# State-space chunks on one core: outputs made as features by tokens in column halves, the decay mask on ScalarE, two banks of transposes

## Chip, cores and metric

The kernel runs on one NeuronCore of one Trainium2 chip. The metric is the time of one launch in device microseconds, the median over several runs of the same kernel. A core has TensorE for matrix products and transposes, VectorE, ScalarE and GpSimd for element work, and SyncE, which here does nothing but start transfers. Products land in PSUM, which has eight banks of 512 float32 columns on 128 partitions; each `[P, 512]` tile below is one bank.

## What is computed

One inference step of a two-layer model: a Mamba-2 state-space (SSD) layer, then a Griffin (RG-LRU) layer, each followed by a squared-ReLU MLP. There are 16 meta tokens and 1024 prompt tokens, and beside them 8 sample tokens with states of their own. The change touches the SSD layer's recurrence over the prompt alone. It runs in chunks of 128 tokens (the 16 meta tokens are a short chunk in front), with 8 groups of 4 heads, 64 features a head and 128 states:

```python
cs = jnp.cumsum(ac, axis=2)                     # a: log decays, per token and head
Lmat = segsum_exp(jnp.moveaxis(cs, 2, -1))      # exp(cs_l - cs_s) where s <= l, else 0
cb = jnp.einsum("bclgn,bcsgn->bcgls", Cc, Bc)
scores = cb[:, :, :, None] * Lmat
y_diag = jnp.einsum("bcgrls,bcsgrp->bclgrp", scores, x)           # x is x * dt
decay_to_end = jnp.exp(cs[:, :, -1:] - cs)
chunk_states = jnp.einsum("bcsgn,bcsgrp->bcgrpn", Bc, x * decay_to_end[..., None])
# h_next = h * exp(cs_last) + chunk_states, h_prev is the state ahead of a chunk
y_off = jnp.einsum("bclgn,bcgrpn->bclgrp", Cc, h_prev) * jnp.exp(cs)[..., None]
y = y_diag + y_off                              # then y + x * d_skip, times silu(z), group norm, w_out
```

Everything around it (projections, convolution, gates, norms, MLPs) is the same in both kernels.

## The kernel before

**Layout.** Activations stand with features on partitions and tokens along the columns. For a group g, `x0` and `x1` are the 2 x 128 features of its four heads after the convolution, `Bf` and `Cf` the 128 state columns; in the trace all four are called `conv`. The result `yf` has the same layout, 2 x 128 features by tokens.

**Order of work.** The SSD layer goes group by group. `ssd_group(g)` is a generator; each step of it (a slot) issues one stage of each of three consecutive chunks. Between the slots the loop over groups advances a second generator, `fill(g)`, which issues the projection of the next group's x, B and C columns and of this group's gate z: bundles of 24 float16 products (8 tiles of the inner dimension, three passes of high and low parts) into one of the four banks `mm0` to `mm3`. The trace calls them `mm<-U,wh`. Further lanes run beside them: the group norm of the group before, and the conversion of weights to float16 parts. The instructions are then placed on their engines by a scheduler that honours data dependences, so the order on an engine isn't exactly that of the code. Every engine call passes through a helper, so nearly every row of the trace names line 89 and is told apart by its tiles.

**A chunk.** Its work in three stages, in the slots i, i+1 and i+2:

- `spread`, a slot earlier: SyncE starts one transfer (line 1017) that copies the chunk's cumulative sums from the DRAM tile `csd` to all 128 partitions, as `L`, 4 heads x 128 columns.
- `pe_a`, `ew_a`: TensorE transposes `x0`, `x1` and `Bf` into the bank `tp` and multiplies B by C into the bank `cb`. VectorE subtracts each token's own sum from `L` and caps at 0 (four instructions, `L<-L,ncs`); ScalarE takes the exponential; VectorE makes `xdt` = x dt and `xdd` = x dt exp(cs_last - cs) out of `tp`, then `cbm` = `cb` times the triangle, then `L` = `L` times `cbm`. ScalarE copies B's transpose to `Bt`.
- `pe_b`, `ew_b`: TensorE makes the chunk's state `st` (`xdd` by `Bt`), and in the bank `yo` the part from the carried state (`hst` by C, tokens on partitions, 256 columns) and four products of `xdt` and `L`, 64 columns each. GpSimd multiplies the carried state by its decay, VectorE adds `st`: the next `hst`. VectorE makes `yt` = first half of `yo` times `es` (exp of the sums, a column per head), and adds the second half.
- `pe_c`, `ew_c`: TensorE transposes `yt` back into free columns of `cb`; VectorE adds x times D and writes `yf`.

`tp`, `cb`, `st` and `yo` have one bank each: the next chunk's products into a bank wait until the last reader of the bank is done. `L`, `xdt`, `xdd`, `yt` and `hst` have two buffers each. In slot 1 the sample tokens' B and C go by way of DRAM to all partitions (`row`, `bcd`, `bc`), in slots 3 to 6 VectorE and GpSimd work on the sample tokens' states, and slot 8 ends them. A float32 product shows as two passes in the trace (f32 x2).

Of the kernel before, what the change touches and what calls it, by code (L numbers as in the profile page):

```python
# [10 lines left out]
F32 = mybir.dt.float32  # L11
# [10 lines left out]
P = 128  # L22
# [55 lines left out]
class Queue:  # L78
    """An engine; while hold is set its instructions are issued in program order, and later ones behind them."""
# [38 lines left out]
class Body:  # L118
# [18 lines left out]
    def tab(self, *args, **kw):  # L137
        """An activation whose function needs a table set: these stay in program order."""
# [13 lines left out]
    # ---------------------------------------------------------------- setup  # L152
    def setup(self):
# [28 lines left out]
        # pre-norm gains and group-norm gains scaled by a power of two so that hi/lo fit float16  # L182
# [13 lines left out]
        # the inputs of the ffn leave room for sums of four  # L196
# [13 lines left out]
        self.csd = self.dram.tile([288, P], F32, name="csd")  # L210
        self.bcd = [self.dram.tile([8, 2, P], F32, name=f"bcd{i}") for i in range(2)]
# [33 lines left out]
    def pow2(self, b, n, pool, tag):  # L245
        """p = the power of two at or below b; s = 2^14 / p."""
# [9 lines left out]
    # -------------------------------------------------------------- weights  # L256
# [14 lines left out]
    def split(self, w, st, s, parts):  # L271
        """w = float16 hi and lo parts of st * s, s [P, parts] by contiguous column ranges."""
# [12 lines left out]
    def wconv(self, st, kind, cols=SW):  # L285
        """A strip of weights as float16 hi and lo parts [P, 2, KT, cols], the factor that undoes its scaling and,
        for kinds h and H, the factor of its hidden units. Kind a takes a bound from the sums of the magnitudes, kind s
        one that kind g found before; kinds 2 and S carry the factors of the hidden rows. Kinds H and S are for the
        products by Winograd's form: with the quarters that are used as they are."""
# [50 lines left out]
    def quarter(self, s, inv):  # L340
        """Scales that leave room for sums of four."""
# [101 lines left out]
    def summed(self, b, s):  # L443
        """Whether the hidden units of a strip of block b enter the second product by Winograd's form."""
# [7 lines left out]
    def bundle(self, ps, w, m, act, c, kts=range(KT), first=True, last=True):  # L452
        """ps += sum over k of w[k, m tile]^T act[k, chunk c], three passes of the float16 parts."""
# [14 lines left out]
    def new_u(self):  # L468
        """Float16 parts of the normed input by chunk and k tile."""
# [28 lines left out]
    def normed(self, x, ss, i, hi, lo, pool):  # L498
        """Steps: the pre-norm i of a chunk (its k tiles in x), as float16 parts in hi and lo [P, KT, n]."""
# [15 lines left out]
    def boundary(self, m, ss, xc, piece, ipost, xdst, ipre, U, pool):  # L515
        """Steps: x + norm(m) for a piece of a chunk to xdst; then its pre-norm."""
# [37 lines left out]
    def last_phase(self, ws, act, ipost, xsrc, xdst, ipre, evac, pre=None, split0=None):  # L554
        """The last product before a norm, chunk by chunk; the norms of a chunk run beside the next one."""
# [47 lines left out]
    def first_phase(self, strips, act, evac):  # L603
        """Products of the first strips after a norm: chunk 2 of the input comes last."""
# [15 lines left out]
    # ------------------------------------------------------------------ SSD  # L620
    def ssd(self):
# [5 lines left out]
        with tc.tile_pool(name="dts", bufs=1) as dts:  # L627
            with tc.tile_pool(name="rows", bufs=1, reuse_waits="tile") as rows, \
# [23 lines left out]
                for g in range(G):  # L652
# [5 lines left out]
                    nslot = 13  # L658
# [29 lines left out]
    def start_x(self, c):  # L688
        """A chunk of the input, in the room of later rows: its k tiles, and room left over."""
# [25 lines left out]
    def start_norm(self, U, c, x, sq, ufs):  # L715
        """Steps: the first pre-norm of a chunk."""
# [942 lines left out]
```

## Time and profile before

| what | value |
|---|---|
| median of 3 runs | 2834.31 us (2834.26, 2834.31, 2837.87) |
| span of the profiled execution | 2836.7 us, 56933 instructions |
| its own time beside the span | not recorded apart; the span is 2.4 us over the median |
| mean granted TensorE clock | 0.968 |
| TensorE products busy | 2583.1 us (91%) |
| VectorE busy | 2110.1 us (74%) |
| ScalarE busy | 1322.6 us (47%) |
| GpSimd busy | 691.4 us (24%) |
| DMA | 229.15 MB, mean 81 GB/s |

"Busy" is the time in which the engine executes something; what it waits for is told by other views. A row of the timeline begins with start and length in us and ends, in brackets, with a wait and what ended it. A row of a group of instructions has, between bars, its total busy time and the mean ns of one, and then the idle time ahead of it. A row by windows has for each engine the busy us and the count of instructions, then the granted clock as a share of the full one, the share of time in which the DMA engines are busy, and GB/s.

### The profile page before, as it was taken

Reading aid. Unit: us, or ns where it says so; the run is one execution under the profiler, and the core shown is the slowest. Engines: PE = TensorE matmul, PEld = TensorE weight load, DVE = VectorE, ACT = ScalarE, POOL = GpSimd, SP = SyncE. Lnnn points to the kernel's source line nnn. Section 1 sums busy time; section 2 is a strip of 40 time slices with the busy share of each in tenths; the row PEclk is TensorE's granted clock in tenths of the full one; section 3 lists DMA queues with packets and bytes.
Section 4 is the critical chain, followed back from the end, with each engine's and each line's share of the span. In section 5 each row is a group of like instructions: output and inputs, shape, how many; then the busy total and the mean of one; then the engine's idle time right before and its main releaser. Section 6 shows DMA issues by size and latency. Waiting matters only on the chain. (4 is left out here: it accounts for less than half of the span.)

```text
span 2836.7 us, 56933 instructions
## 1 busy us (share of the span) xinstructions
PE 2583.1 (91%) x23209; PEld 2060.6 (73%) x23209; DVE 2110.1 (74%) x5043; ACT 1322.6 (47%) x2148; POOL 691.4 (24%) x972
## 2 busy tenths in 40 slices
PE   4999999999999999789989999979999779989998
PEld 2666666666666667789989976646667779989976
DVE  4889778977873685568778788787685667878776
ACT  4655455545544354344253344658564335253352
POOL 2222111212212024442232201123014452231301
PEclk9999999999999999889999999989999989999999
DMA  3232233223345320101122123110220101111122
GB/s 123 99 119 90 87 107 115 102 88 108 113 159 187 117 106 31 46 31 46 61 72 79 46 110 113 63 62 33 89 108 31 46 31 46 47 45 53 54 73 95
DMA packets 52758, 229.15 MB, mean 81 GB/s; under 512 B 9056, under 2 KB 18416, under 8 KB 31632
## 3 DMA queue, kind: packets, MB, share of 16 engines
q1 hardware_dynamic: 46112, 190.81, 19.1%
q0 software_dynamic: 6384, 34.71, 3.1%
q8 instruction: 181, 2.97, 0.4%
q14 instruction: 81, 0.66, 0.1%
HBM read 186.28 MB, written 39.22 MB: 79 GB/s over the span
## 5 line engine op out<-in xcount | busy, mean ns | idle before, releaser
L89 PEld LDWEIGHTS <-wh 128*128 128x128 f16 x17040 | 1504.0, 99 | 503.7 <-issue 54.7
L89 PE MATMUL mm<-U,wh 128*128 128x350 f16 (+3 forms) x7056 | 989.4, 297 | 20.7 <-ACT rr L89 13.2
L89 PE MATMUL mm<-H,wh 128*128 128x175 f16 (+5 forms) x5664 | 557.7, 253 | 35.3 <-DVE z L89 30.4
L89 PEld LDWEIGHTS <-wp 128*128 128x128 f16 x3888 | 311.0, 99 | 87.6 <-issue 60.5
L89 POOL TENSOR_TENSOR ws<-ws 128x256 f32<-128x256 f32 (+1 forms) x192 | 205.2, 1069 | 328.6 <-DVE wp L89 214.4
L89 DVE TENSOR_TENSOR z<-z,mm 128x175 f32<-128x175 f32 (+3 forms) x648 | 228.4, 370 | 29.2 <-ACT z L89 22.0
L89 POOL PARTITION_ALL_REDUCE wgb<-rm x100 | 55.5, 555 | 656.6 <-issue 338.4
L89 PE MATMUL mm<-U,wp 128*128 128x175 f16 (+1 forms) x1728 | 154.8, 245 | 55.2 <-DVE z L89 55.1
L89 PE MATMUL mm<-TT,wh 128*128 128x175 f16 (+1 forms) x1728 | 167.0, 248 | 10.2 <-ACT TT L89 9.3
L89 ACT ACTIVATE z<-z,ti 128x700 f32<-128x700 f32 (+1 forms) x72 | 63.0, 875 | 183.5 <-DVE z L89 183.5
L89 DVE SCALAR_TENSOR_TENSOR wh<-ws,sw,wh 128x1024 f16<-128x1024 f32 x94 | 122.0, 1320 | 28.3 <-ACT wh L89 28.3
L89 DVE TENSOR_SCALAR qw<-wgb 128x1 f32<-128x1 f32 x103 | 15.5, 150 | 167.3 <-POOL wgb L89 167.1
L89 DVE SCALAR_TENSOR_TENSOR wh<-ws,s,wh 128x256 f16<-128x256 f32 x256 | 114.7, 490 | 11.1 <-ACT wh L89 11.1
L89 DVE TENSOR_REDUCE rm<-ws 128x1 f32<-128x2048 f32 x40 | 91.3, 2281 | 31.2 <-DMA ws<-w 26.7
L89 PE MATMUL mm<-H,wp 128*128 128x175 f16 (+1 forms) x864 | 90.5, 241 | 25.5 <-DVE z L89 23.1
L89 DVE TENSOR_TENSOR ss<-ss,sqt 128x350 f32<-128x350 f32 (+3 forms) x154 | 75.9, 500 | 41.8 <-ACT sqt L89 41.1
L89 ACT ACTIVATE wh<-ws,s 128x512 f16<-128x512 f32 x128 | 83.0, 710 | 48.0 <-POOL ws L89 23.2
L89 DVE SCALAR_TENSOR_TENSOR conv<-pre,ssmall,conv 128x1072 f32<-128x1072 f32 x78 | 103.8, 1330 | 0.1
L89 ACT ACTIVATE wh<-ws,sw 128x2048 f16<-128x2048 f32 x47 | 93.7, 1993 | 14.5 <-DVE sw L89 11.7
L89 DVE TENSOR_SCALAR L<-L,ncs 128x128 f32<-128x128 f32 (+1 forms) x288 | 90.6, 357 | 13.2 <-DMA L<-csd 13.2
L89 DVE TENSOR_TENSOR H<-z,H 128x175 f16<-128x175 f32 (+5 forms) x120 | 81.2, 694 | 23.6 <-ACT H L89 19.5
L89 ACT ACTIVATE pre<-mm,undo 128x8 f32<-128x8 f32 (+1 forms) x104 | 46.5, 474 | 110.7 <-PE mm L89 110.7
(279 smaller groups left out, 4176.9 us busy)
## 6 DMA issues: line engine op xcount, KB each, us to landing
ws<-w SPq DMA_DIRECT2D x64, 1024.0 KB, 4.9
ws<-w_ssd_in SPq DMA_DIRECT2D x24, 1024.0 KB, 5.4
L<-csd SPq DMA_DIRECT2D x64, 256.0 KB, 3.2
ws<-w_lru_in SPq DMA_DIRECT2D x12, 1024.0 KB, 4.9
xd<-xc POOLq DMA_DIRECT2D x6, 1400.0 KB, 5.5
xc<-xd SPq DMA_DIRECT2D x6, 1400.0 KB, 6.0
h<-ssd_h SPq DMA_DIRECT2D x8, 1024.0 KB, 4.9
bc<-bcd SPq DMA_DIRECT2D x8, 1024.0 KB, 4.8
```

Source lines behind the costliest of these rows:

```text
L89: r = f(*args, **kw)
```

## The change

1. `y` is made directly as features by tokens. The part from the carried state becomes two products of 128 columns, with two heads of `hst` stationary and C moving. The four products of `xdt` and `L` exchange their operands: `xdt` (64 columns) is stationary, `L` (128 columns) moves, and head h lands on partitions 0 to 63 or 64 to 127 of `yo`, by h modulo 2. The two transposes of `yt`, and the third stage with them, are gone; a group has 10 slots of chunk work and `nslot` is 12.
2. The exponentials of the sums, formerly columns `es`, are now needed along the tokens: they are written to a second DRAM tile, `esd`, and spread over the partitions by two transfers a chunk into `ex`, issued by SyncE in `spread`. VectorE multiplies the first half of `yo` by `ex`; GpSimd adds that to `yf`, into which VectorE has written x D + the second half of `yo`.
3. The mask: four Relu on ScalarE of cs - `L` (scale -1, the sum as bias), then the exponential with scale -1, in place of four instructions on VectorE.
4. `tp` alternates between two banks (those formerly `tp` and `cb`), and B C goes to its last 128 columns.

```diff
+        self.esd = self.dram.tile([288, P], F32, name="esd")
...
-                    nslot = 13
+                    nslot = 12
...
-        ncs = dts.tile([P, 9, 32], F32, name="ncs")
-        nc.vector.tensor_scalar(f(ncs), f(cs), -1.0, None, op0=OP.mult)
+        esr = dtt.tile([96, 3, 128], F32, name="esr")
+        self.tab(esr, csr, AF.Exp)
+        nc.sync.dma_start(self.esd.rearrange("(i p) c -> p i c", i=3), esr)
...
-        es = dts.tile([P, 9, 32], F32, name="es")
-        self.tab(f(es), f(cs), AF.Exp)
...
-        nc.vector.tensor_tensor(f(dd), f(ncs), tps[:, :288], op=OP.add)
+        nc.vector.tensor_tensor(f(dd), tps[:, :288], f(cs), op=OP.subtract)
...
-        def pe_a(i, cb):
+        def pe_a(i):
...
-            tp = psp.tile([P, 512], F32, tag="tp", name="tp")
+            tp = psp.tile([P, 512], F32, tag=("tp", "cb")[i % 2], name="tp")
...
-            nc.tensor.matmul(cb[:Q, :Q], Bf[:, es], Cf[:, es], start=True, stop=True)
+            nc.tensor.matmul(tp[:Q, 384:384 + Q], Bf[:, es], Cf[:, es], start=True, stop=True)
...
             nc.sync.dma_start(L[:Q, :, :Q], self.csd[None, r:r + 4, :Q].to_broadcast([Q, 4, Q]))
             S["L", i] = L
+            if i:
+                ex = tmp.tile([P, 2, 128], F32, tag="yt", name="ex", bufs=2)
+                for h in range(2):
+                    nc.sync.dma_start(ex[64 * h:64 * h + 64], self.esd[None, r + h:r + 4:2].to_broadcast([64, 2, 128]))
+                S["ex", i] = ex
...
             for h in range(4):
-                nc.vector.tensor_scalar(L[:Q, h, :Q], L[:Q, h, :Q], self.ncs[:Q, tt, 4 * g + h:4 * g + h + 1], 0.0,
-                                        op0=OP.add, op1=OP.min)
-            self.tab(L[:Q, :, :Q], L[:Q, :, :Q], AF.Exp)
+                nc.scalar.activation(L[:Q, h, :Q], L[:Q, h, :Q], AF.Relu, scale=-1.0,
+                                     bias=self.cs[:Q, tt, 4 * g + h:4 * g + h + 1])
+            self.tab(L[:Q, :, :Q], L[:Q, :, :Q], AF.Exp, scale=-1.0)
...
             if i:
-                nc.tensor.matmul(yo[:, :256], Cf[:, es], fl(hst[0]), start=True, stop=True)
+                for t in range(2):
+                    nc.tensor.matmul(yo[:, 128 * t:128 * t + 128], fl(hst[0][:, 2 * t:2 * t + 2]), Cf[:, es], start=True,
+                                     stop=True)
             for h in range(4):
-                nc.tensor.matmul(yo[:Q, 256 + 64 * h:320 + 64 * h], L[:Q, h, :Q], xdt[:Q, h], start=True, stop=True)
+                p, o = 64 * (h % 2), 256 + 128 * (h // 2)
+                nc.tensor.matmul(yo[p:p + 64, o:o + Q], xdt[:Q, h], L[:Q, h, :Q], start=True, stop=True)
...
                 nc.gpsimd.tensor_tensor(hn, hst[0], self.ecd[:, tt, hs, None].to_broadcast([P, 4, 64]), op=OP.mult)
                 nc.vector.tensor_tensor(fl(hn), fl(hn), st[:, :256], op=OP.add)
-                nc.vector.tensor_tensor(yt.rearrange("p (h d) -> p h d", h=4),
-                                        yo[:, :256].rearrange("p (h d) -> p h d", h=4),
-                                        self.es[:, tt, hs, None].to_broadcast([P, 4, 64]), op=OP.mult)
-                nc.vector.tensor_tensor(yt, yt, yo[:, 256:], op=OP.add)
...
-        def pe_c(i, cb):
-            Q = dims(i)[0]
-            yt = S.pop(("y", i))
-            for t in range(2):
-                nc.tensor.transpose(cb[:, 128 + 128 * t:128 + 128 * t + Q], yt[:Q, 128 * t:128 * t + 128],
-                                    ident[:Q, :Q])
...
             for t in range(2):
                 nc.vector.scalar_tensor_tensor(yf[:, t, c0:c0 + Q], xs[t][:, es], v["dsk"][:, 2 * g + t:2 * g + t + 1],
-                                               cb[:, 128 + 128 * t:128 + 128 * t + Q], op0=OP.mult, op1=OP.add)
+                                               yo[:, 256 + 128 * t:256 + 128 * t + Q], op0=OP.mult, op1=OP.add)
+            if i:
+                ex = S.pop(("ex", i))
+                nc.vector.tensor_tensor(fl(ex), yo[:, :256], fl(ex), op=OP.mult)
+                nc.gpsimd.tensor_tensor(yf[:, :, c0:c0 + Q], yf[:, :, c0:c0 + Q], ex, op=OP.add)
```

The rest of the diff removes comments.

The order of the instructions moves with it. The numbers behind the names of tiles are buffers; `conv_2896` (before) and `conv_2881` (after) are the same group's C, `conv_2269`, `conv_2520`, `conv_2730` its x0, x1, B (after: `conv_2265`, `conv_2468`, `conv_2726`). On TensorE, one chunk's block in the middle of the third group, before:

```order
L89 MATMUL cb_3320<-ident_83,yt_3265 128x128 x2
L89 MATMUL st_3323<-xdd_3271,Bt_3279 128x256
L89 MATMUL yo_3325<-hst_3264,conv_2896 128x256
L89 MATMUL yo_3325<-xdt_3270,L_3162 128x64 x4
L89 MATMUL tp_3331<-ident_83,conv_2269 128x128
L89 MATMUL tp_3331<-ident_83,conv_2520 128x128
L89 MATMUL tp_3331<-ident_83,conv_2730 128x128
L89 MATMUL cb_3320<-conv_2896,conv_2730 128x128
```

and after:

```order
L89 MATMUL st_3312<-xdd_3260,Bt_3268 128x256
L89 MATMUL yo_3314<-conv_2881,hst_3252 128x128 x2
L89 MATMUL yo_3314<-L_3149,xdt_3259 64x128 x4
L89 MATMUL tp_3321<-ident_83,conv_2265 128x128
L89 MATMUL tp_3321<-ident_83,conv_2468 128x128
L89 MATMUL tp_3321<-ident_83,conv_2726 128x128
L89 MATMUL tp_3321<-conv_2881,conv_2726 128x128
```

The transposes of `yt` are gone, the two products into `yo` have their operands exchanged, and all that the next chunk's first stage needs comes out of one bank. Between two such blocks of a group stand 24 to 49 projection products after the change.

On SyncE, the same group's transfers in the order in which they are issued, before:

```order
L1017 DMA L_3162<-csd_142 128x512
L1090 DMA bcd0_143<-row_3198 8x256
L1093 DMA bc_3201<-bcd0_143 128x2048
L1017 DMA L_3244<-csd_142 128x512
L1017 DMA L_3318<-csd_142 128x512
L1017 DMA L_3413<-csd_142 128x512
L1017 DMA L_3487<-csd_142 128x512
```

and after:

```order
L1023 DMA ex_3235<-esd_143 64x2x128 x2
L1018 DMA L_3307<-csd_142 128x512
L1018 DMA L_3428<-csd_142 128x512
L1023 DMA ex_3309<-esd_143 64x2x128 x2
L1023 DMA ex_3430<-esd_143 64x2x128 x2
L1018 DMA L_3509<-csd_142 128x512
L1018 DMA L_3609<-csd_142 128x512
L1018 DMA L_3694<-csd_142 128x512
L1023 DMA ex_3511<-esd_143 64x2x128 x2
```

`L_3307` and `ex_3309` belong to one chunk, `L_3428` and `ex_3430` to the next, `L_3509` and `ex_3511` to the one behind: `ex` of a chunk stands behind `L` of up to two later chunks.

On ScalarE, the middle of the same group, after (before, one exponential of `L` stands in the place of each row of Relus and the exponential behind it):

```order
L89 ACTIVATE L_3307<-L_3307,cs_945 128x128 x3
L89 ACTIVATE L_3307<-L_3307 128x512
L89 ACTIVATE pre_3355<-mm_3402,undo_3105 128x350
L89 ACTIVATE ysp_3142<-yf_2039 128x2x350
L89 ACTIVATE L_3428<-L_3428,cs_945 128x128 x2
L89 ACTIVATE Bt_3463<-tp_3442 128x128
L89 ACTIVATE L_3428<-L_3428,cs_945 128x128 x2
L89 ACTIVATE L_3428<-L_3428 128x512
```

`Bt_3463` belongs to the chunk of `L_3307`; it now stands behind the first Relus of the next chunk's `L_3428`, which wait for the landing of its sums.

More of the change, by code (lines that the diff above doesn't have):

```diff
@@ L840, in dt_phase @@
         self.dtfm, self.decfm = fm
-        self.dt, self.cs, self.ncs, self.ecd, self.es, self.dtd = dt, cs, ncs, ecd, es, dtd
+        self.dt, self.cs, self.ecd, self.dtd = dt, cs, ecd, dtd
     def softplus(self, out, x, pool, n, parts=1):
@@ L1018, in spread, with ew_a @@
             S["L", i] = L
-        def ew_a(i, tp, cb):
+            if i:
[3 more added lines that the diff above has]
+                S["ex", i] = ex
+        def ew_a(i, tp):
             Q, tt, es, _ = dims(i)
@@ L1034, in ew_a @@
             cbm = tmp.tile([P, 128], F32, tag="cbm", name="cbm", bufs=2)
-            nc.vector.tensor_tensor(cbm[:Q, :Q], cb[:Q, :Q], tri[:Q, :Q], op=OP.mult)
+            nc.vector.tensor_tensor(cbm[:Q, :Q], tp[:Q, 384:384 + Q], tri[:Q, :Q], op=OP.mult)
             nc.vector.tensor_tensor(L[:Q, :, :Q], L[:Q, :, :Q], cbm[:Q, None, :Q].to_broadcast([Q, 4, Q]),
@@ L1046, in pe_b @@
             if i:
-                nc.tensor.matmul(yo[:, :256], Cf[:, es], fl(hst[0]), start=True, stop=True)
+                for t in range(2):
+                    nc.tensor.matmul(yo[:, 128 * t:128 * t + 128], fl(hst[0][:, 2 * t:2 * t + 2]), Cf[:, es], start=True,
+                                     stop=True)
             for h in range(4):
-                nc.tensor.matmul(yo[:Q, 256 + 64 * h:320 + 64 * h], L[:Q, h, :Q], xdt[:Q, h], start=True, stop=True)
+                p, o = 64 * (h % 2), 256 + 128 * (h // 2)
+                nc.tensor.matmul(yo[p:p + 64, o:o + Q], xdt[:Q, h], L[:Q, h, :Q], start=True, stop=True)
             return st, yo
         def ew_b(i, st, yo):
-            Q, tt, es, _ = dims(i)
+            Q, tt, es, c0 = dims(i)
             hn = tmp.tile([P, 4, 64], F32, tag="hst", name="hst", bufs=2)
-            yt = tmp.tile([P, 256], F32, tag="yt", name="yt", bufs=2)
             if i == 0:
                 nc.vector.tensor_copy(fl(hn), st[:, :256])
-                nc.vector.tensor_copy(yt[:Q], yo[:Q, 256:])
             else:
@@ L1061, in ew_b @@
                 nc.vector.tensor_tensor(fl(hn), fl(hn), st[:, :256], op=OP.add)
-                nc.vector.tensor_tensor(yt.rearrange("p (h d) -> p h d", h=4),
-                                        yo[:, :256].rearrange("p (h d) -> p h d", h=4),
-                                        self.es[:, tt, hs, None].to_broadcast([P, 4, 64]), op=OP.mult)
-                nc.vector.tensor_tensor(yt, yt, yo[:, 256:], op=OP.add)
-            hst[0] = hn
-            S["y", i] = yt
-        def pe_c(i, cb):
-            Q = dims(i)[0]
-            yt = S.pop(("y", i))
-            for t in range(2):
-                nc.tensor.transpose(cb[:, 128 + 128 * t:128 + 128 * t + Q], yt[:Q, 128 * t:128 * t + 128],
-                                    ident[:Q, :Q])
-        def ew_c(i, cb):
-            Q, tt, es, c0 = dims(i)
             for t in range(2):
                 nc.vector.scalar_tensor_tensor(yf[:, t, c0:c0 + Q], xs[t][:, es], v["dsk"][:, 2 * g + t:2 * g + t + 1],
-                                               cb[:, 128 + 128 * t:128 + 128 * t + Q], op0=OP.mult, op1=OP.add)
+                                               yo[:, 256 + 128 * t:256 + 128 * t + Q], op0=OP.mult, op1=OP.add)
[3 more added lines that the diff above has]
+                nc.gpsimd.tensor_tensor(yf[:, :, c0:c0 + Q], yf[:, :, c0:c0 + Q], ex, op=OP.add)
+            hst[0] = hn
         def sample_bc():
@@ L1126, in ssd_group @@
         spread(0)
-        for i in range(n + 2):
+        for i in range(n + 1):
             if i + 1 < n:
                 spread(i + 1)
-            cb = psp.tile([P, 512], F32, tag="cb", name="cb")
-            if 0 <= i - 2 < n:
-                pe_c(i - 2, cb)
-            if 0 <= i - 1 < n:
+            if i:
                 rb = pe_b(i - 1)
             if i < n:
-                ra = pe_a(i, cb)
-            if 0 <= i - 2 < n:
-                ew_c(i - 2, cb)
-            if 0 <= i - 1 < n:
+                ra = pe_a(i)
+            if i:
                 ew_b(i - 1, *rb)
             if i < n:
-                ew_a(i, ra, cb)
+                ew_a(i, ra)
             if i == 1:
```

## The prediction

> **What bounds the kernel now.** I read first the busy times of three stretches of the span, the middle one being the state-space chunks (from the first group's slots to the last's), because only there does the change touch anything.
>
> ```profile
> span 2836.7 us, 56933 instructions
> core 0: us, PE busy (x) PEld busy (x) DVE busy (x) ACT busy (x) POOL busy (x), PEclk, DMA share, GB/s
> 115.90:850.00 734.10, 696.82 (x4642) 491.02 (x4641) 601.42 (x1679) 371.62 (x571) 154.46 (x259) 0.98 0.31 109
> 392.90:487.90 95.00, 89.90 (x611) 63.10 (x610) 78.31 (x213) 48.98 (x77) 19.47 (x35) 1.00 0.29 103
> ```
>
> The stage takes 734 us. TensorE is busy for 697 of them, 95%; VectorE for 601, 82%; ScalarE for 372, 51%; GpSimd for 154, 21%. The last row is one group of heads, 95.0 us, with the same shares. So TensorE sets the pace, and VectorE is close behind. TensorE's idle time is 734.1 - 696.8 = 37.3 us, and the granted clock of 0.98 stands for about 0.02 x 734 = 15 us of further loss. Second I read whom TensorE waits for in that stretch (total us, times, longest):
>
> ```profile
> PE cb L89 <- DVE cbm L89: 12.8, 9, 3.0
> PE yo L89 <- DVE yt L89: 7.1, 5, 2.8
> PE yo L89 <- DVE L L89: 6.6, 3, 3.2
> PE st L89 <- DVE hst L89: 4.8, 6, 1.1
> PE st L89 <- ACT Bt L89: 2.6, 7, 1.4
> ```
>
> Four rows name VectorE: 12.8 + 7.1 + 6.6 + 4.8 = 31.3 of the 37.3 us. A saving thus comes in two ways: fewer TensorE cycles in a chunk (worth their full length) and fewer of these waits. Third, the order of time on TensorE in an undisturbed chunk (start, length of the merged row, which overlaps the next row by the tail of the last matmul, so starts are what I subtract):
>
> ```profile
> 406.48 0.38 PE L89 MATMUL cb<-ident,yt 128*128 128x128 f32 x2
> 406.70 0.60 PE L89 MATMUL st<-xdd,Bt 128*128 128x256 f32 x2
> 407.13 0.59 PE L89 MATMUL yo<-hst,conv 128*128 128x256 f32 x2
> 407.56 1.00 PE L89 MATMUL yo<-xdt,L 128*128 128x64 f32 x8
> 408.40 0.50 PE L89 MATMUL tp<-ident,conv 128*128 128x128 f32 x3
> 408.74 0.39 PE L89 MATMUL cb<-conv 128*128 128x128 f32 x2
> 408.96 3.72 PE L89 MATMUL mm<-U,wh 128*128 128x350 f16 x24
> ```
>
> A chunk's block is 2.48 us (406.48 to 408.96), and a bundle of 24 projection products follows. There are 8 groups x 8 full chunks = 64 blocks. Each float32 product stands as two passes.
>
> **The change on TensorE.** (1) The two transposes of `yt` go: 406.48 to 406.70, 0.22 x 64 = 14 us. They stand on TensorE itself, so this counts in full. (2) The product with the carried state was one of 256 columns in two passes, 0.43 us (407.13 to 407.56); it becomes two of 128 columns, four passes. The `cb<-conv` row, 128 columns in two passes, takes 0.22, so four take 0.44: nothing. (3) The products of mask and x exchange their operands: eight passes with 64 moving and 128 stationary columns become eight with 128 moving and 64 stationary ones, in halves of the array that alternate. Now they take 0.84 (407.56 to 408.40), 0.105 a pass. One after the other, the new ones take 8 x 0.11 = 0.88, a loss of 0.04; with the two halves fully beside each other half of that, a gain of 0.40. No row shows two halves at work. Changes of the array's layout have two near rows, in a group's first chunk:
>
> ```profile
> 394.70 0.69 PE L89 MATMUL st<-xdd,Bt 16*128 16x256 f32 x2 [0.21 <-ACT Bt L89]
> 395.32 0.61 PE L89 MATMUL yo<-xdt,L 16*16 16x64 f32 x8
> 396.25 0.39 PE L89 MATMUL cb<-conv 128*128 128x128 f32 x2
> 396.47 0.38 PE L89 MATMUL mm<-ident,conv 128*8 128x128 f32 x2
> 396.69 0.61 PE L89 MATMUL mm<-U,wh 128*128 128x350 f16 x3
> ```
>
> Going to 8 stationary columns and back costs nothing: 0.22, as the row before it. Going from `st` to 16 rows takes 0.62 from start to start where two such passes take 0.43, so a change costs at most 0.19. Two changes a block give a worst end of 0.04 + 0.38 = 0.42 x 64 = 27 us lost; the best end is 0.40 x 64 = 26 us gained. The 8-column row is the nearest (columns are narrowed here too), so I put changes at nothing and the halves between 0 and 26, at 10 gained: the two passes of a head must follow each other, so only neighbours of different heads can meet.
>
> The Trainium skill ("TensorEngine Tiling (Array Packing)", Key Properties) says that a change of tiling mode drains the engine, and that tiles run in parallel. The 0.22 above shows no drain. By the parallel part alone this term would be 26; by the drain alone it would lie towards the other end.
>
> **The change on the other engines.** (4) VectorE loses the four subtractions that prepare the mask and the two steps that make `yt`, and gains one product with the spread exponentials `ex`.
>
> ```profile
> 406.91 0.87 DVE L89 TENSOR_SCALAR L<-L,ncs 128x128 f32<-128x128 f32 x4
> L89 DVE TENSOR_TENSOR yt<-yo,es 128x256 f32<-128x256 f32 x64 | 26.7, 417 | 18.0 <-issue 9.6 <-PE yo L89 5.6 <-ACT wh L89 2.6
> L89 DVE TENSOR_TENSOR yt<-yt,yo 128x256 f32<-128x256 f32 x64 | 26.1, 409 | 0.0
> L89 POOL TENSOR_TENSOR hst<-hst,ecd 128x256 f32<-128x256 f32 x64 | 42.1, 658 | 125.3 <-DVE hst L89 51.4 <-DVE ysp L89 22.0 <-PE mm L89 15.6
> L89 ACT ACTIVATE Bt<-tp 128x128 f32<-128x128 f32 x64 | 17.3, 270 | 23.4 <-DVE xdd L89 22.9
> ```
>
> Per chunk 0.87 + 0.42 + 0.41 - 0.42 = 1.28 us, x 64 = 82 us less of VectorE's 601. (5) GpSimd gains one addition of 128x256 a chunk, priced as its state product: 64 x 0.66 = 42 us, on an engine at 21%. It stands in GpSimd's queue beside the state product that the next chunk needs; the states stand ahead of the additions there in most places, so I charge nothing directly. But GpSimd holds VectorE up:
>
> ```profile
> 455.05 3.61 POOL L89 TENSOR_TENSOR h<-h,decfm 128x2048 f32<-128x2048 f32 x1 [1.98 <-DMA h<-ssd_h]
> 455.13 3.55 DVE L89 SCALAR_TENSOR_TENSOR yf<-conv,ssmall,ys 128x8 f32<-128x8 f32 x1
> ```
>
> An 8-column operation takes 3.55 us because a GpSimd product runs beside it. The new additions may hold VectorE between 0 and 42 us in all; I take 8, since VectorE is reading PSUM, or idle, for much of a chunk. So VectorE gets about 74 us back. The Trainium skill ("GPSIMD Engine Reference", Key points) states the rule: GpSimd shares its SBUF interfaces with VectorE, in the way of operations with two SBUF inputs. The pair of rows agrees; were every addition to fall on such an operation, the relief would be 40 instead of 74.
>
> (6) ScalarE gains four Relu of 128x128 a chunk. Priced as `Bt`, of that size: 4 x 0.27 = 1.08, x 64 = 69 us, and it would be busy 441 of some 690 us, 64%. That is hidden as long as a chunk's exponentials are done before its mask is needed, one bundle and one block later (3.7 + 2.5 = 6.2 us); relu and exp take 1.08 + 0.63. What is queued behind the first Relu, which waits for its rows to land, are `Bt` and the copies out of the projection's banks; `Bt` is what TensorE's `st` waits for. (7) SP gets two more transfers a chunk. The landing time is that of the present rows:
>
> ```profile
> L<-csd SPq DMA_DIRECT2D x64, 256.0 KB, 3.2
> ```
>
> They move 128 KB a chunk, half of that row. SP issues nothing else that the chunks wait for but `L`, so the issuing is hidden; their place in the queue is the first rival below. The stage's DMA share is 0.31, so bandwidth is no limit. (8) `tp` with two banks and no `cb`: the first wait of the list above, 12.8 us, is the wait for the single bank of `cb`, and loses its cause. Late next is what stands behind it in the same chunk, `st` and `yo`, which still have one bank each and are freed by VectorE. (9) The start-up gains one exponential and one small transfer and loses a multiplication and an exponential: nothing. (10) One slot fewer (12 for 13) only moves projection products among slots.
>
> **The waits.** Their ends are 0 (VectorE still too late in the slots that also carry the sample tokens, the convolution and the group norm) and 31 + 15 = 46 us (all of VectorE's share and of the clock's). VectorE gives back 74 us, more than twice its 31, but TensorE becomes shorter too, and the heavy slots stay heavy: I take about half, 24 us.
>
> **Sum.** 14 + 0 + 10 + 24 = 48 us; the second bank of `tp` has no entry beside its part of the waits. The profiled execution's span is 2836.7; the runs shown are 2834.26, 2834.31 and 2837.87, so the span lies 2.4 above their median, and nothing else of that execution's time is recorded. 2836.7 - 48 = 2788.7 by the profile, 2834.3 - 48 = 2786 on the scale of the median.
>
> **Rivals.**
> A. The late rows: slower. In the new order of SP `ex` of a chunk stands behind `L` of chunks up to two later, and each of those waits for TensorE to have read a mask. `ex` then lands 3.2 us after that. VectorE takes its work in order, so its product with `ex` blocks everything behind it, and `yo`, with its one bank, stays occupied. The price is up to 3.2 us a chunk less what VectorE does in between. From 48 / 64 = 0.75 us a chunk on TensorE the gain is gone. At 1.0 us in each of 64 chunks the time is 2834 - 48 + 64 = 2850. For it: three or four of a group's eight chunks stand so. Against it: 24 to 49 projection products, 3.7 to 7.6 us by the row of 24 above, stand between two chunks in the new order, as long as the landing or longer. Chance 0.10.
> B. The waits stay. VectorE is over-full in the middle slots, and what it sheds is taken up by ScalarE's and GpSimd's new places in the chain: only 14 + 10 = 24 us come, 2810. For it: `Bt` now stands behind Relus that wait for a landing. Chance 0.25.
> C. All of it: 14 + 26 + 38 (most of the 46) = 78 us, 2756. For it: 82 us off the engine that TensorE waits for, and halves that run together. Chance 0.20.
> D. The halves lose and the waits stay: 14 gained, 14 lost to layout changes at half their upper price. 2834, no change. Chance 0.06.
> Forecast, 2775 to 2800: chance 0.39.
>
> **Numbers.** Predicted 2786. The range leaves out A (0.10), the lower tail of C and the upper half of D: 2748 to 2828. A measurement of this kernel can tell about 0.2%, 6 us, from no change. Faster: forecast, B, C and a bit of D, 0.86; the same 0.05; slower: A less its mild end, 0.09.
>
> **What the new profile would show.** Right: no `cb<-ident,yt`; a block of about 2.1 us from `st` to the first projection product; the `yo<-L,xdt` passes stepping 0.055 to 0.11; VectorE at some 525 busy us in the stage, ScalarE at 440, GpSimd at 200; TensorE's waits for VectorE about 15 us. Wrong: VectorE idle behind a landing of `ex`; `st` waiting for `Bt`; steps around the halves longer than 0.2 us; VectorE's operations stretched beside the new additions.

## The result and the profile after

The change made the kernel slower: 2882.28 us (median of 4 runs, 2879.68 to 2887.62) against 2836.09 (4 runs), a ratio of 1.0161 (95% interval 1.0147 to 1.0176). The forecast was 2786, with a range of 2748 to 2828. The profiled execution has a span of 2885.9 us, 49.2 more than that of before. From the start of the first `st` to that of the last, 40.8 of these arise (748.0 us against 707.2), and 8.4 in all the rest of the kernel, nearly all of which is the same code. Within six groups (from the second group's first `st` to the eighth's), which is the same work in both, the row of before and then that of after, in the columns of the prediction's first fence:

```profile
197.40:776.50 579.10, 550.31 (x3654) 385.74 (x3654) 469.72 (x1281) 294.24 (x457) 118.71 (x206) 0.98 0.30 104
```

```profile
203.50:810.40 606.90, 544.45 (x3642) 363.44 (x3642) 423.41 (x1014) 355.15 (x673) 158.90 (x256) 0.95 0.33 109
```

Busy time times clock is TensorE's work at full speed: 550.31 x 0.98 = 539 us before and 544.45 x 0.95 = 517 after. So the work did shrink, by 22 us. But TensorE's idle time grew from 28.8 to 62.5 us, 34 more, and what the granted clock took from its busy time grew from 11 to 27 us, 16 more (the clock is given to 0.01, so that this is good to some 4 us). -22 + 34 + 16 = +28, the difference of the two rows. VectorE shed 46 us and TensorE's pace did not follow it.

An undisturbed chunk after the change, start and length on TensorE:

```profile
412.74 0.59 PE L89 MATMUL st<-xdd,Bt 128*128 128x256 f32 x2
413.17 0.61 PE L89 MATMUL yo<-conv,hst 128*128 128x128 f32 x4
413.70 0.66 PE L89 MATMUL yo<-L,xdt 128*64 128x128 f32 x8
414.29 0.55 PE L89 MATMUL tp<-ident,conv 128*128 128x128 f32 x3
414.68 0.39 PE L89 MATMUL tp<-conv 128*128 128x128 f32 x2
414.90 0.31 PE L89 MATMUL mm<-U,wh 128*128 128x348 f16 x1
```

The block is 2.16 us (412.74 to 414.90) against 2.48: that part of the forecast came true. Where the time went is in TensorE's waits in the chunks' stage (total us, times, longest):

```profile
PE st L89 <- ACT Bt L89: 29.5, 21, 4.2
PE yo L89 <- DVE ex L89: 24.4, 13, 3.1
PE yo L89 <- DVE L L89: 14.1, 17, 1.6
PE st L89 <- DVE hst L89: 5.4, 5, 2.5
```

The wait for `cbm`, at the head of the list before, is gone. In its place stands a wait for ScalarE's `Bt`, 29.5 us against 2.6, and one for VectorE's `ex`, 24.4. What these two wait for in their turn, on ScalarE and VectorE, and then in SyncE's queue of transfers:

```profile
ACT L L89 <- DMA L<-csd: 90.2, 41, 5.1
...
DVE cbm L89 <- ACT Bt L89: 28.0, 23, 3.1
...
DVE ex L89 <- DMA ex<-esd: 10.7, 6, 3.3
```

```profile
SPq L1018 <- DVE L L89: 178.2, 37, 11.9
SPq L1018 <- PE yo L89: 162.2, 60, 11.6
...
SPq L1023 <- POOL yf L89: 101.0, 25, 7.6
```

ScalarE stands 90.2 us in front of Relus whose sums have not landed. (A wait of this length is no loss by itself: in e8 below it is 92.6 us, and that kernel is not slower than before.) SyncE stands 101.0 us at line 1023, the transfer of `ex`, for a GpSimd addition to give a buffer back. One such place, from the timeline of all engines (POOL is GpSimd, SPq the issue on SyncE):

```profile
427.04 0.93 POOL L89 PARTITION_ALL_REDUCE wgb<-rm  x1 [6.71 <-ACT rstd L89]
...
435.01 0.88 POOL L89 TENSOR_TENSOR yf<-yf,ex 128x256 f32<-128x256 f32 x1 [6.92 <-PE st L89]
435.92 2.85 SPq L1023 DMA_DIRECT2D ex<-esd  x4
436.79 0.73 POOL L89 TENSOR_TENSOR yf<-yf,ex 128x256 f32<-128x256 f32 x1
438.87 0.53 SPq L1018 DMA_DIRECT2D L<-csd  x1
...
442.47 1.28 ACT L89 ACTIVATE L<-L,cs 128x128 f32<-128x128 f32 x4 [2.05 <-DMA L<-csd]
442.56 0.41 DVE L89 TENSOR_TENSOR xdd<-tp,dtd 128x256 f32<-128x256 f32 x1
...
443.80 0.26 ACT L89 ACTIVATE Bt<-tp 128x128 f32<-128x128 f32 x1
444.12 0.92 PE L89 MATMUL st<-xdd,Bt 128*128 128x256 f32 x2 [3.21 <-ACT Bt L89]
```

And the stretch that follows:

```profile
445.52 0.51 POOL L89 PARTITION_ALL_REDUCE wgb<-rm  x1 [6.00 <-ACT gsq L89]
...
448.53 8.75 SPq L1018 DMA_DIRECT2D L<-csd  x2
...
451.93 0.99 ACT L89 ACTIVATE L<-L,cs 128x128 f32<-128x128 f32 x3 [3.68 <-DMA L<-csd]
...
453.37 0.67 POOL L89 TENSOR_TENSOR yf<-yf,ex 128x256 f32<-128x256 f32 x1 [7.34 <-issue]
...
454.21 0.26 ACT L89 ACTIVATE Bt<-tp 128x128 f32<-128x128 f32 x1
...
454.50 0.29 DVE L89 TENSOR_TENSOR cbm<-tp,tri 128x128 f32<-128x128 f32 x1 [3.08 <-ACT Bt L89]
454.52 0.70 PE L89 MATMUL st<-xdd,Bt 128*128 128x256 f32 x2 [1.11 <-ACT Bt L89]
...
454.89 0.73 POOL L89 TENSOR_TENSOR yf<-yf,ex 128x256 f32<-128x256 f32 x1
...
456.22 0.66 PE L89 MATMUL yo<-L,xdt 128*64 128x128 f32 x8 [0.26 <-DVE L L89]
...
457.45 3.04 SPq L1023 DMA_DIRECT2D ex<-esd  x3
```

Read both downwards. The first addition comes late, behind a PARTITION_ALL_REDUCE (the maximum over the partitions that sets the scale of a weight strip) and 6.92 us of idle time. It ends at 435.89, and only then is `ex` transferred (435.92), and only behind it the next `L` (438.87). It lands at 442.4, the Relus run, `Bt` follows, and TensorE has stood 3.21 us for `st`. (Its other input, `xdd`, was ready only at 442.97, so the Relus ahead of `Bt` account for 1.15 us of these at most; in the second stretch `xdd` was ready long before `Bt`.) `L` has two buffers, which TensorE frees by its mask products: the transfer at 448.53 waited for those of the chunk that was late at 444.12, its Relus start 3.68 us late, and `Bt` and `cbm` with them, and so the mask products at 456.22. A late mask makes the sums after it late: it is a loop.

The next reduction, at 445.52, has a row of 0.51 us, but GpSimd does nothing else from 439.5 to 453.4: 6.0 us idle ahead of it and 7.3 behind. The additions behind it are over at 455.62, though, and `ex` is issued at 457.45: here SyncE stood at the second `L` of line 1018, until TensorE had read the mask (456.88). That is the place that rival A named. This `ex` lands at 463.6, and VectorE waits for it.

Such a landing of `ex` on which VectorE stands occurs six times (the row `DVE ex <- DMA ex` above), once in each of the six middle groups. I followed the stage back from its last `st` to its first, at each step to what ended last: the chain passes over these six landings, 33.6 us in all. The same walk meets no landing of `ex` in e1, e3, e4 and e10 below, 6.0 us in e2 and 5.1 in e13.

The same gaps stood in the profile of before, where no addition of `ex` was queued behind them:

```profile
434.87 0.82 POOL L89 PARTITION_ALL_REDUCE wgb<-rm  x1 [5.90 <-issue]
442.82 0.91 POOL L89 TENSOR_TENSOR gsq<-gsq 128x348 f32<-128x348 f32 x1 [7.13 <-issue]
```

The Trainium skill ("GPSIMD Engine Reference", Instruction dispatch) says that the first call to a freshly loaded kernel on GpSimd costs about 6 us that no instruction of the profile shows. The 5.90 and 6.00 us ahead of the reductions agree. Behind them stand another 7.1 to 7.3 us.

### The profile page after: what moved, and what is told of

Same layout as the page of the kernel before. It is cut to its first block, busy times and chain, and to the rows that moved or that the text cites. A ratio compares the mean times of both kernels' runs of the same rounds, so it can differ in the third digit from the quotient of the medians.

```text
span 2885.9 us, 57203 instructions
## 1 busy us (share of the span) xinstructions
PE 2571.2 (89%) x23193; PEld 2025.2 (70%) x23193; DVE 2050.4 (71%) x4682; ACT 1403.1 (49%) x2436; POOL 743.0 (26%) x1036
## 5 line engine op out<-in xcount | busy, mean ns | idle before, releaser
L89 ACT ACTIVATE L<-L,cs 128x128 f32<-128x128 f32 (+1 forms) x288 | 92.3, 380 | 109.2 <-DMA L<-csd 90.2
L89 DVE SCALAR_TENSOR_TENSOR conv<-pre,ssmall,conv 128x1072 f32<-128x1072 f32 x78 | 120.3, 1543 | 9.6 <-ACT conv L89 9.2
L89 POOL TENSOR_TENSOR yf<-yf,ex 128x256 f32<-128x256 f32 x64 | 51.4, 803 | 177.4 <-issue 86.1
```

Source lines behind the costliest of these rows:

```text
L89: r = f(*args, **kw)
```

## The experiments

All times below are ratios to the kernel before, run beside them on the same chip; 0.1% is 2.8 us. "Six groups" is the stretch of the first two rows, from each profile: 579.1 us before, 606.9 after.

### Who holds the queue

Theory Q: GpSimd's reductions hold the additions, these the buffers of `ex`, these SyncE's queue. Rivals: the mask on ScalarE (M), and GpSimd's additions slowing VectorE (C). One rival can't be excluded by a time alone: the scheduler places the instructions anew for each kernel, so that an edit of one line also changes the order elsewhere. Of the 829 instructions of ScalarE in after's stage, the longest sequence that stands in the same order is 707 in e1, 629 in e2 and 720 in e13. No run changes the order and leaves the rest.

First, the addition on VectorE:

```diff
-                nc.gpsimd.tensor_tensor(yf[:, :, c0:c0 + Q], yf[:, :, c0:c0 + Q], ex, op=OP.add)
+                nc.vector.tensor_tensor(yf[:, :, c0:c0 + Q], yf[:, :, c0:c0 + Q], ex, op=OP.add)
```

> The addition of `ex` to `yf` moves from GpSimd to VectorE, all else as after. Theory Q (the queue): GpSimd does nothing else for some 13 us around each PARTITION_ALL_REDUCE (6.0 us idle ahead of the one at 445.52, 7.3 behind it); additions that stand behind it keep the two buffers of `ex`, SyncE waits for them, the next `L` waits on SyncE behind `ex`, and ScalarE's Relu, `Bt` and TensorE's `st` wait for `L`. Then the waits fall back to about those of before while TensorE's shorter block stays: 2800 to 2835 us. Rival M (the mask on ScalarE is the trouble): `Bt` stays late, 2865 or more. Rival C (GpSimd's additions slow VectorE's operations): a part comes back, 0.3 us of stretch a chunk less 0.42 for the addition, so 2870 to 2890.

Measured 2823.09 us, 0.9954 (0.9936 to 0.9971): the loss is gone, and a gain of 0.46% is there. Six groups: 554.3 us, in a profiled execution that was the fastest of the five (2813 us). Its row:

```profile
202.50:756.80 554.30, 525.14 (x3644) 350.12 (x3643) 427.54 (x1057) 357.06 (x682) 120.65 (x206) 0.99 0.36 118
```

TensorE's work at full speed is 525.14 x 0.99 = 520 us, as in after; idle time is 29.2 us, as in before. VectorE took over an addition of 0.475 us in each of 48 chunks, 23 us, and is busy only 4 us longer than in after. Is the difference C? One line of the convolution in before, after and this kernel (total us, mean ns):

```profile
L89 DVE SCALAR_TENSOR_TENSOR conv<-pre,ssmall,conv 128x1072 f32<-128x1072 f32 x78 | 103.8, 1330 | 0.1
```

```profile
L89 DVE SCALAR_TENSOR_TENSOR conv<-pre,ssmall,conv 128x1072 f32<-128x1072 f32 x78 | 120.3, 1543 | 9.6 <-ACT conv L89 9.2
```

```profile
L89 DVE SCALAR_TENSOR_TENSOR conv<-pre,ssmall,conv 128x1072 f32<-128x1072 f32 x78 | 103.3, 1324 | 6.9 <-ACT conv L89 6.9
```

In after this line is 16.5 us longer. But four of its 78 steps make up 13.4 of that, and they run beside another GpSimd product, that of the sample tokens' states, which every kernel has. The step that starts at 468.93 takes 4.68 us beside this row:

```profile
468.61 3.87 POOL L89 TENSOR_TENSOR h<-h,decfm 128x2048 f32<-128x2048 f32 x1 [2.59 <-DMA h<-ssd_h]
```

In before it is other operations that fall beside this product, as the prediction shows. Where the additions stay on GpSimd and `h` meets no step of the convolution, the mean is 1395 ns (e2), 1323 (e3) and 1340 (e13). Over all of VectorE's operations that overlap an addition, I estimate the stretch from the trace of after (their length less the median of their kind) at some 18 us. So C is there, but it can't be the loss: in e2 the same estimate gives 22 us.

Second, the additions stay on GpSimd, but `ex` has four buffers:

```diff
-                ex = tmp.tile([P, 2, 128], F32, tag="yt", name="ex", bufs=2)
+                ex = tmp.tile([P, 2, 128], F32, tag="yt", name="ex", bufs=4)
```

> Four buffers of `ex` instead of two; the additions stay on GpSimd, and all else is as after. Q: SyncE no longer waits for an addition held up behind a reduction, so most of the loss comes back: 2800 to 2845. M: no change, 2870 to 2885. C: no change, 2875 to 2885.

(The tile `row`, which shares the tag, gets four as well.) 2834.73 us, 1.0005 (0.9992 to 1.0018); six groups 562.0. Two buffers of 1 KB a partition bring back nearly all that was lost. C can't explain that, and neither can M. Yet SyncE waits longer for additions than in after, not shorter as was expected:

```profile
SPq L1023 <- POOL yf L89: 174.1, 33, 12.9
```

So the sum of SyncE's waits is no measure of the harm; what counts is whether a chunk waits for what stands behind. And the order has moved: in after an addition of `ex` is the first instruction behind 22 of the 24 gaps that follow a reduction, in e2 behind 5, in e13 behind 11.

Third, the mask:

```diff
-                nc.scalar.activation(L[:Q, h, :Q], L[:Q, h, :Q], AF.Relu, scale=-1.0,
-                                     bias=self.cs[:Q, tt, 4 * g + h:4 * g + h + 1])
-            self.tab(L[:Q, :, :Q], L[:Q, :, :Q], AF.Exp, scale=-1.0)
+                nc.vector.tensor_scalar(L[:Q, h, :Q], L[:Q, h, :Q], self.cs[:Q, tt, 4 * g + h:4 * g + h + 1], 0.0,
+                                        op0=OP.subtract, op1=OP.min)
+            self.tab(L[:Q, :, :Q], L[:Q, :, :Q], AF.Exp)
```

> The mask goes back to four instructions on VectorE a chunk, all else as after. Q: `L` still lands late, and now it is VectorE that stands still for it, with 56 us more work: 2875 to 2910. M: the trouble goes: 2800 to 2835. C: as Q, since the additions stay.

2851.85 us, 1.0063 (1.0044 to 1.0083): about 1% better than after, which neither Q nor M had. Q was incomplete: by this run, the late sums need the Relus ahead of `Bt` on ScalarE to do their full harm. A loss of 0.6% stays.

Fourth and fifth, the reduction itself left out in the first layer's strips, in after and in before:

```diff
-        nc.gpsimd.partition_all_reduce(gb, gmax, P, RED.absmax)
+        if own:
+            nc.gpsimd.tensor_copy(gb, gmax)
+        else:
+            nc.gpsimd.partition_all_reduce(gb, gmax, P, RED.absmax)
```

> As after, but the reduction over the partitions that finds the scale of a weight strip of the first layer is left out (GpSimd copies the partition's own maximum instead), so GpSimd has no gap of 13 us in the chunks' stage. Q: the additions are prompt, and the time is below that of before with the same piece left out, by 15 to 50 us: about 2790 to 2825. M and C: it stays above it by 30 or more: 2865 or more.

> As before, but with the reduction over the partitions of the first layer's weight strips left out in the same way. In the kernel before, what stands on GpSimd behind a reduction is the carried state's decay alone. Q: little changes, 2820 to 2836, so that the order of the two kernels turns round when the reductions are out. M and C: also 2820 to 2836, but the order doesn't turn.

After without the reductions takes 2791.24 us, 0.9846 (0.9827 to 0.9866), before without them 2809.98, 0.9918 (0.9891 to 0.9945). So the order of the two kernels turns round, as Q says: 0.9846 / 0.9918 = 0.993, about 20 us in favour of the change. That before gains too, more than expected, is work that waits for GpSimd there as well; its first `st` starts at 115.5 us instead of 127.3.

Does it turn also when the maximum is found in another way and nothing is left out? In both kernels, TensorE transposes the column, VectorE takes the maximum of the row, and a product with ones spreads it:

```diff
+            nc.tensor.transpose(ps[:1, :128], gmax, self.ident)
+            nc.vector.tensor_reduce(gr, ps[:1, :128], axis=AX.X, op=OP.max)
+            nc.tensor.matmul(ps[:, 128:129], self.ones[:1, :], gr, start=True, stop=True)
+            nc.vector.tensor_copy(gb, ps[:, 128:129])
```

> As after, additions on GpSimd, but the maximum over the partitions for the first layer's weight strips is found by TensorE and VectorE (transpose of one column, maximum along the row, product with a row of ones), so that GpSimd has no reduction in the chunks' stage; nothing is left out. Theory Q: near the run that left the reduction out (2791 us): 2788 to 2812. If the loss lay in VectorE's or ScalarE's load, the added VectorE steps bring no gain: 2865 or more.

> The kernel before with the same replacement. By the run that left the reduction out (2810 us): 2805 to 2825. With e10 it shows what the change is worth where GpSimd is prompt: Q says 10 to 25 us faster.

> As e1_add_dve (2823 us), with the same replacement of the reduction. If the reductions cost beyond the additions of `ex` (they also delay the carried state's decay and the first strips), 2785 to 2810; if e1 has taken all that there was, 2815 to 2828.

2829.54 us, 0.9984 (0.9975 to 0.9994), and for before 2842.07, 1.0025 (1.0011 to 1.0039). 0.9984 / 1.0025 = 0.996: with GpSimd prompt, the change is a gain of some 12 us. The replacement costs more than was expected, since it adds a chain of TensorE and VectorE steps of its own; on e1 (e11: 2829.07, 0.9982, 0.9968 to 0.9995) it takes away more than half of what e1 had gained.

### A link that was not foreseen

In before, `cb` had a bank of its own. Now B C lies in the bank of the transposes, and the readers of one bank take turns in the order of the code: `xdd` on VectorE, then `Bt` on ScalarE, then `cbm` on VectorE. That is the row `DVE cbm <- ACT Bt`, 28.0 us, which the profile of before does not have. The Trainium skill ("PSUM — Partial Sum Buffer", PSUM bank collisions raise a hardware error) says that two engines may not touch one bank in the same partitions at once, reads included, and that the compiler's scheduler puts a dependency between two such instructions. The row agrees. The edit puts `cbm` ahead of `Bt`, on after and on e1:

```diff
-            Bt = tmp.tile([P, 128], F32, tag="Bt", name="Bt", bufs=2)
-            nc.scalar.activation(Bt[:Q], tp[:Q, 256:384], AF.Copy)
             cbm = tmp.tile([P, 128], F32, tag="cbm", name="cbm", bufs=2)
             nc.vector.tensor_tensor(cbm[:Q, :Q], tp[:Q, 384:384 + Q], tri[:Q, :Q], op=OP.mult)
+            Bt = tmp.tile([P, 128], F32, tag="Bt", name="Bt", bufs=2)
+            nc.scalar.activation(Bt[:Q], tp[:Q, 256:384], AF.Copy)
```

> As after, with two lines exchanged: `cbm` is made ahead of `Bt`. In the trace of after VectorE waits 28.0 us (23 times) with `cbm` for ScalarE's `Bt`, a row that before does not have: `cbm` and `Bt` now read one bank, and its readers take turns. Theory T (turns): VectorE no longer stands behind ScalarE there; that row goes, and 8 to 25 us come back: 2857 to 2874. Rival L (the turns only fill time in which the mask would wait for its late sums anyway): 2876 to 2888.

> As e1_add_dve (2823 us), with the same exchange. There the row of `cbm` waiting for `Bt` has 17.6 us. T: 2805 to 2816, since TensorE waits for what VectorE makes next. L: 2819 to 2828, since `Bt` now comes after `cbm`, and TensorE's `st` waits for `Bt` (19.6 us in e1) as long or a little longer.

On after it brings 1.0002 (0.9991 to 1.0013; 2840.75 us): two lines exchanged, and the whole loss of 1.6% is gone, more than was expected of it. (With them the order on GpSimd changed, as said above, so not all of it need be the turn in the bank.) In its waits the row of `cbm` is gone, and the turn stands the other way round:

```profile
ACT Bt L89 <- DVE cbm L89: 23.8, 15, 3.1
...
PE st L89 <- ACT Bt L89: 19.6, 20, 2.8
PE yo L89 <- DVE ex L89: 14.7, 10, 2.3
```

On e1, where the loop was cut already, the same exchange is of no use: 0.9984 (0.9972 to 0.9996) against 0.9954, worse than both theories had it. So the loss was a loop, GpSimd's addition to `ex` to `L` to Relu to `Bt` to `cbm` to the mask to the buffers of `L`. Its start is shown: without reductions or without the addition on GpSimd it is gone (e1, e4 with e5, e10 with e12), and the landings of `ex` leave the chain. That e2 and e13 cut it at the buffers of `ex` and at `cbm` fits, but their order changed too, and e3, which takes out the Relus, ends only 1.0 of the 1.6%.

### What the change is worth without the loop

Mask alone, in before, with nothing else changed:

> The kernel before with nothing changed but the mask, as four Relu on ScalarE. By the prediction's fourth and sixth steps VectorE is relieved of 56 us and ScalarE has room: 2815 to 2828. By M2: `Bt` and the copies out of the projection's banks come late behind the Relus: 2850 to 2870. Theory B lies between: a little later for `Bt`, a little earlier for VectorE: 2828 to 2842.

2828.9 us, 0.9986 (0.9972 to 0.9999). VectorE's busy time in the stage falls from 601 to 529 us, and the kernel gains 4 us. TensorE's longest waits:

```profile
PE st L89 <- ACT Bt L89: 15.1, 22, 2.7
PE yo L89 <- DVE yt L89: 9.6, 13, 2.2
PE yo L89 <- DVE L L89: 3.1, 1, 3.1
PE st L89 <- DVE hst L89: 2.7, 3, 2.0
```

The waits that name VectorE did fall, from 31.3 to 15.4 us. But the one for `Bt` rose from 2.6 to 15.1: what VectorE gave back, the Relus ahead of `Bt` took. This is rival B of the prediction, seen alone. What VectorE's relief would be worth without the Relus, no run shows.

The mask back on VectorE in e1:

> As e1_add_dve, with the mask back on VectorE too. e3 gained 30 us on the kernel after by that alone. Theory B: Relus that wait for a landing no longer stand ahead of `Bt` on ScalarE, but VectorE waits for that landing and has 0.87 us a chunk more: the two about cancel, 2812 to 2832. Theory M2 (the mask on ScalarE costs 30 us whatever holds the queue): 2788 to 2800. Rival V (VectorE is the bound again): 2835 to 2850.

0.9963 (0.995 to 0.9976), as e1 with the mask on ScalarE: 44 us more of VectorE in the six groups, no time. Without the loop the mask's place is worth nothing on balance. A third buffer of `L` in e1 (tag `L` with `bufs=3`), and one bank of transposes instead of two (`tag="tp"` in every slot):

> As e1_add_dve (2823 us), with three buffers of `L` instead of two. In e1 TensorE's `st` waits 19.6 us in the stage for `Bt`, which stands on ScalarE behind Relus that wait 52 us for landings of `L`. Theory B (the buffers of `L`): the sums are there earlier, so the wait for `Bt` goes: 2798 to 2812. Rival X (`Bt` is late since VectorE is late with `xdd` and the tiles before it): 2818 to 2828.

> As e1_add_dve, with one bank of transposes instead of two (the second bank stays unused). By the prediction's eighth step the second bank takes away a wait of some 12.8 us: 2833 to 2845. If the wait had already moved elsewhere, no change: 2818 to 2828.

0.9951 (0.9933 to 0.9968) and 0.9948 (0.9932 to 0.9965): neither matters. With the third buffer the wait for `Bt` falls from 19.6 to 6.6 us, and that for `ex` rises from 8.2 to 24.3; with one bank the wait for `cbm`, 12.8 us in before, is 1.4:

```profile
PE tp L89 <- DVE cbm L89: 1.4, 3, 0.7
```

Then both `cbm` first and three buffers, and `Bt` copied by VectorE (`nc.vector.tensor_copy`), with two and with three buffers of `L`:

> As e14, with three buffers of `L`. If the two waits, the turns and the late sums, cover each other (either alone bought little), both together give 2795 to 2812; if TensorE is held by VectorE's own length in the slots with the sample tokens, 2815 to 2825.

> As e1_add_dve, with B's transpose copied out of the bank by VectorE instead of ScalarE, so that all readers of that bank are on one engine and none stands behind a Relu. In e1 `st` waits 19.6 us for ScalarE's `Bt` and `cbm` 17.6 us; VectorE gains some 0.28 us a chunk, 18 us. If these waits are worth their length less the copy, 2800 to 2815 (0.988 to 0.993 of before); if VectorE's order decides and not ScalarE, no gain: 2818 to 2832.

> As e17, with three buffers of `L` as well, so that the sums are earlier and SyncE comes sooner to the transfers of `ex` behind them. If what is left in e17 is the wait for the mask, some 5 to 15 us less than e17; if it is VectorE's order, the same as e17 within 5 us.

0.9967 (0.9956 to 0.9977), 0.9988 (0.9971 to 1.0005) and 0.9929 (0.9906 to 0.9952). Taken off ScalarE, `Bt` is waited for on VectorE: in e17 (whose profiled execution was the slowest of ten, 2846 us)

```profile
PE st L89 <- DVE Bt L89: 36.0, 22, 4.1
```

and 12.4 us in e18, the best of the kernels that leave nothing out, though its interval meets those of e1, e6, e9 and e16. e15 is slower than either of its two theories had it. The wait moves, and its sum stays: why the six groups keep 29 us or more of TensorE's idle time in each of these orders (32.7 in e18, 39.0 in e6) is not settled.

Last, the two halves of the partitions. The order of the heads' products in e1 is made 0, 2, 1, 3:

> As e1_add_dve, but the four heads' products are issued in the order 0, 2, 1, 3, so that neighbours land in the same half of the partitions, apart from one pair. In the kernel after, the eight passes take 0.59 us from start to start of the next group of products (before: 0.84). If the halves run beside each other, the neighbours now can't: 0.11 a pass for most, 0.75 to 0.90 us, and 10 to 20 us more in the whole, 2833 to 2843. If something else shortened them, no change: 0.59 us and 2818 to 2828.

0.9948 (0.9933 to 0.9963), and the passes take the same time, 506.40 to 507.00:

```profile
506.40 0.67 PE L89 MATMUL yo<-L,xdt 128*64 128x128 f32 x8
507.00 0.55 PE L89 MATMUL tp<-ident,conv 128*128 128x128 f32 x3
```

Single records show passes in pairs in either order, mostly 6 to 14 ns apart, and the pairs 0.10 to 0.11 us apart behind the first (that one 0.16). That the halves work beside each other fits; the run was to take this away and did not, so how neighbours of one half are paired stays open.

## Why the prediction was wrong, step by step

- **TensorE's block** (steps 1 to 3): 24 us forecast, (2.48 - 2.16) x 64 = 20 measured. The transposes gave 0.22 as said. The halves gave 0.25 a chunk, 16 us, where 10 were taken. The steps around them are longer: `yo<-conv,hst` takes 0.53 for four passes, where 0.44 was forecast, and the transposes 0.39 for 0.34. So a change of layout costs 0.05 to 0.1, within the bound of 0.19, where I had put nothing. The two statements of the Trainium skill on tiling ("TensorEngine Tiling (Array Packing)", Key Properties), a drain at a change of mode and tiles in parallel, both fit these lengths, but e9 did not confirm the second, and why the 8-column row showed no cost is not shown.
- **VectorE's relief** (steps 4 and 5): 74 us of 64 chunks would be 55 in 48; 46 came. The stretch beside GpSimd's additions, taken at 8 us, is some 18 by the estimate above, within the bounds of 0 and 42.
- **The step that failed is 5**: "on an engine at 21% ... so I charge nothing directly". GpSimd's share of busy time left out its gaps: 13 us of idle time around each reduction, though rows with 5.9 and 7.1 us of idle time stood in the profile of before. What is queued behind a reduction is late by that, and the change queued there the one instruction that frees the buffers of a transfer. Step 7 then called SyncE's issuing hidden without asking what its next `L` stands behind. What was put at nothing here cost some 57 us: 1.0161 for the two kernels as they are against 0.996 with GpSimd prompt (e10 and e12), and e1 gives 59.
- **Step 8** saw two banks where one had been, and not that `cb` had lost its own: `cbm` came to wait for ScalarE. The second bank itself is worth nothing (e16).
- **The waits' term**, 24 us: with the loop cut, the idle time in six groups is 29.2 us, before 28.8. So the term is 0 where 24 was taken. That relief of VectorE would shorten TensorE's idle time was inferred from the engine named in the waits. In e8 the waits that name VectorE fall by 16 us, and that for ScalarE's `Bt` grows by 12: the step left out that the relief came by way of the engine that makes `Bt`. What is shown is a chain of latencies through ScalarE, VectorE and the banks, whose last link changes its name with each edit.
- **Rivals**: A, late `ex` and a blocked VectorE, had the sign and the place (24.4 us of `yo` waiting for `ex`), with a chance of 0.10 and 2850 us. Its mechanism was half right: SyncE's order did it, and at 457.45 `ex` stands behind an `L` that waits for TensorE, as A has it. But what made that mask late was GpSimd, and the price had neither `Bt` (29.5 us) nor the clock (16 us in six groups). B named the Relus ahead of `Bt`, and priced them as lost gain, not as loss. Of the signs of being wrong, three came: `st` waiting for `Bt`, VectorE idle behind a landing of `ex` (10.7 us), and VectorE's operations stretched. With the loop cut, e1 gains 12 to 13 us of the 48 forecast.

## What to carry to other kernels

Before work is moved to an engine because it is idle, read its timeline and not its share: what stands ahead of the new instruction in its queue, how long the gaps around its special instructions are, and which buffers, and so which transfers, its end sets free. When a product moves into another's bank, look at which engines read that bank and in which order: their readers now wait for each other. And a wait that names an engine says who was last, not that the engine is full; take the load off in a single edit first, as e8 does, before a gain is booked on it, and look there at which wait has taken its place. Where a scheduler places the instructions, compare the orders of two kernels before a difference is put down to the line that was edited.

## What the runs showed of the hardware

A PARTITION_ALL_REDUCE whose row has 0.5 to 0.8 us stands in some 14 us of GpSimd's time (5.90 + 0.82 + 7.13, and 6.00 + 0.51 + 7.34); at most a short copy or the like is recorded right behind it, as at 427.85, with the gap behind that. With the reductions of the first layer out (e4), the additions' idle time falls from 177.4 to 36.9 us. A convolution step of 1.33 us took 4.68 beside a GpSimd product of 128x2048. Products that use halves of the array's columns start in pairs, mostly within 14 ns, whether or not neighbours in the code lie in different halves; by the steps around them, a change to that layout and back cost some 0.1 us. The late chain was paid twice: with TensorE idle for 62.5 of 606.9 us instead of 28.8 of 579.1, its mean granted clock fell from 0.98 to 0.95. The two need not go together, though: e7 has 35.8 us of idle time in 558.1 and a clock of 1.00, e15 39.6 in 576.0 and 0.96.
